# Layer A of a two-layer decoder step: every eighth weight block's low half is subtracted on GpSimd instead of VectorE

## The chip, the core and the metric

The kernel runs on one core of one Trainium2 chip. The metric is the device time of one execution in microseconds (us); lower is better. Five engines run in parallel, each through its own instructions in a fixed order: TensorE (PE, with its weight loads as PEld), VectorE (DVE), ScalarE (ACT), GpSimd (POOL) and SyncE (SP, which here issues the DMA transfers). An instruction waits on semaphores for what it reads and for the buffers that it writes, and everything behind it on its engine waits with it.

## The reference

One inference step of a trunk with two layers, D_MODEL = 2048, branch width 4096, 64 heads of 64. It runs on a prompt of 16 + 256 tokens and on 8 single-token samples, 280 token columns in all, with shared weights, all in fp32. Layer A is RWKV-7 time mixing, layer B window attention. What matters here is layer A:

```python
rkvz = jnp.einsum('btpd,pde->btpe', xm[:, :, :4], w_rkvz)     # four weights, 2048 x 4096 each
r, k, v, z = rkvz[:, :, 0], rkvz[:, :, 1], rkvz[:, :, 2], rkvz[:, :, 3]
...
def rwkv7_step(S, inp):
    r, d, k, v, kk, b = inp
    sa = jnp.einsum('bhij,bhj->bhi', S, kk)
    S = S * d[:, :, None, :] - sa[..., None] * b[:, :, None, :] + v[..., None] * k[:, :, None, :]
    return S, jnp.einsum('bhij,bhj->bhi', S, r)
...
y = y.reshape(B, T, WIDTH).astype(dt) * jax.nn.silu(z)
return y @ w_out, S_fin.astype(S0.dtype), xn[:, -1]
```

The outputs are the normalised rows of prompt and samples, the recurrent and shift states, and the key and value caches.

## The kernel before

**Weights.** Every large product keeps its weights on TensorE in two parts, since an fp32 value is multiplied as a high part and a rest: `whi` is the weight rounded to the type fp32r, and `wlo` is the weight minus `whi`. `mm3` (L218 to L220) then issues three matmuls per tile: `whi` by the high part of the activations (L218), `whi` by their rest (L219), and `wlo` by the high part (L220). Weights come in blocks of 128 partitions x 512 elements: two slices of 128 rows of the weight, 256 columns wide. `wunits` makes one block at a time: a DMA on SP's queue into a tile `raw` (L211, five buffers), and then `split`: ScalarE casts `raw` into `whi` (L195) and VectorE subtracts `raw` minus `whi` into `wlo` (L197). `whi` and `wlo` have five buffers each. A buffer of `raw` is free for its next DMA when both the cast and the subtraction have read it.

**Products.** A product of layer A covers 256 output columns and all 2048 rows of depth, so it consumes eight blocks, numbered in tile names by the row slice they start at (0, 2, ... 14; `wlo_z_14` is the eighth block of a product of z). In the stage that matters here `products` (L709) emits 16 products of r, 12 of k, 12 of v, 16 of z (the first four of k and v are made ahead of it), and eight products of the output projection that are named `oa`: 64 products of eight blocks. Each block gives 12 matmuls. In the trace's names `ps_r`, `ps_k`, `ps_v`, `ps_z`, `ps_o` are the PSUM tiles of these products.

**What runs between.** `drive` (L610) steps through the products and, between the pieces, through streams of other work on each group of heads. `prep` loads k, r and v back from DRAM (`kT`, `kk`, `rT`, `vT`) and makes decays; its L932 copies the eight sample columns of six tiles into a tile `sm` on GpSimd, each as its tile comes in. `prep_e` and `scores` build masked score matrices; at L1064 to L1067 GpSimd masks them (`nd`, `N`, `Noff`). Then VectorE turns one of them around and runs a substitution of 14 steps (`stmp` L1075, `NL` L1077), which ends in the transpose `TN` (L1081). `solve` (L1102, `ps_so`) reads `TN` on TensorE. `chain` carries the state over, and `group_norm` ends with transposes `ps_yt` (L1275) that VectorE evacuates into `vT` (L1276). Eight pairs of head groups go through this.

**What sets the order.** TensorE's order is written by hand: `drive` works inside `pe_order`, and TensorE keeps the order in which the program emits. The order on all other engines is chosen when the program is built, by a scheduler that simulates the engines. A block is made one or more blocks ahead of its use, as far as the five buffers allow.

Of the kernel before, what the change touches and what calls it, by code (L numbers as in the profile page):

```python
# [12 lines left out]
F32 = mybir.dt.float32  # L13
# [3 lines left out]
ALU = mybir.AluOpType  # L17
# [81 lines left out]
class Pools:  # L99


    def __init__(self, pools, tags):
        self.pools, self.tags = pools, tags.split()
# [6 lines left out]
class Kernel:  # L110
    def __init__(self, nc, tc, I, O):
        self.nc, self.tc, self.I, self.O = nc, tc, I, O

        self.raws, self.los = [], []

        self.wx = self.hold = None
        self.behind = []
        self.plan = []
        self.pools = {}
# [69 lines left out]
    def dram(self, name, shape):  # L189
        return self.dp.tile(shape, F32, name=name, tag=name)  # L190

    def split(self, hi, lo, src):

        with self.tc.issue_after(self.root) if self.hold else contextlib.nullcontext():
            self.nc.scalar.copy(hi, src)  # L195
        with self.tc.issue_after(self.hold) if self.hold else contextlib.nullcontext():
            return self.nc.vector.tensor_tensor(lo, src, hi.bitcast(F32), op=ALU.subtract)  # L197

    def wunits(self, w, name, nk, col, nc_, per):

        nc = self.nc
        assert nc_ == 256 and per == 2, (nc_, per)
        for k0 in range(0, nk, per):
            t = lambda n, dt, **k: self.wp.tile([128, 512], dt, tag=n, name=f"{n}_{name}_{col}_{k0}", **k)[
                :, :per * nc_].rearrange("p (k c) -> p k c", k=per)
            if self.wx and len(self.raws) % 2:
                raw = self.wx.tile([128, 512], F32, tag="rawx", bufs=4, name=f"raw_{name}_{col}_{k0}")[
                    :, :per * nc_].rearrange("p (k c) -> p k c", k=per)
            else:
                raw = t("raw", F32, bufs=5)  # L210
            self.raws.append(nc.sync.dma_start(raw.rearrange("p k c -> p (k c)"), w[col // 256, k0 // 2]))  # L211
            hi, lo = t("whi", F32R), t("wlo", F32R)
            self.los.append(self.split(hi, lo, raw))
            yield k0, hi, lo

    def mm3(self, ps, wh, wl, xh, xl, start, stop):
# [392 lines left out]

    def drive(self, products, streams, begun, ahead=2000):  # L610
        self.samples = False
        live = [[g, *begun.get(g, (0, None))] for g in streams]

        now = streams[:2]
        more = True
        with self.pe_order():
            while more or self.later or len(live) > 1:
                for s in list(live):
                    if s[1] <= self.pos and (s[2] is None or s[2]()):

                        turn = self.tc.issue_after(self.los[-2].ins) if self.pos and s[0] not in now else \
                            contextlib.nullcontext()
                        try:
                            with self.tc.high_priority(offset=ahead if s[0] is now[1] else 0), turn:
                                w = next(s[0])
                        except StopIteration:
                            live.remove(s)
                            continue
                        w, need = w if isinstance(w, tuple) else (w, None)
                        s[1:] = [self.pos + w, need]  # L630
                live += [[g, 0, None] for g in self.side]
                self.side = []
                more = more and next(products, None) is not None
                self.pos += 1

    def mark(self, *k):
        self.done[k] = self.pos
# [1335 lines left out]
```

## Time and profile before

| | |
|---|---|
| time, median of 3 runs | 2118.64 us (2115.4 to 2123.16) |
| the profiled execution's own time | 2118.32 us, span 2116.5 us, clock 0.99 |
| TensorE busy | 2064.9 us, 98% of the span |
| VectorE busy | 1697.8 us, 80% |
| ScalarE busy | 1263.8 us, 60% |
| GpSimd busy | 122.5 us, 6%, 188 instructions |

The span is the profiled part of that execution; its own time includes what lies around it, 1.8 us. A row of a timeline gives start and duration in us, the engine, the line, and, in brackets, how long the engine had been idle before the instruction and what ended the idle time. A row of the waits gives the engine and line that waited, after the arrow what it waited for, and then the total in us, how many times, and the longest. Rows of a tile or line give duration in ns (minimum, median, maximum) and the first and the last start. Layer A's products run from about 142 to 1275 us.

### The profile page before, as it was taken

Reading aid. Unit: us, or ns where it says so; the run is one execution under the profiler, and the core shown is the slowest. Engines: PE = TensorE matmul, PEld = TensorE weight load, DVE = VectorE, ACT = ScalarE, POOL = GpSimd, SP = SyncE. Lnnn points to the kernel's source line nnn. Section 1 sums busy time; section 2 is a strip of 40 time slices with the busy share of each in tenths; the row PEclk is TensorE's granted clock in tenths of the full one; section 3 lists DMA queues with packets and bytes.
Section 4 is the critical chain, followed back from the end, with each engine's and each line's share of the span. In section 5 each row is a group of like instructions: output and inputs, shape, how many; then the busy total and the mean of one; then the engine's idle time right before and its main releaser. Section 6 shows DMA issues by size and latency. Waiting matters only on the chain.

```text
span 2116.5 us, 55871 instructions
## 1 busy us (share of the span) xinstructions
PE 2064.9 (98%) x21420; PEld 1965.8 (93%) x21420; DVE 1697.8 (80%) x4112; ACT 1263.8 (60%) x2790; POOL 122.5 (6%) x188
## 2 busy tenths in 40 slices
PE   9999999899999999999999999999999999999997
PEld 7999899889899989899999999999999999999997
DVE  8867777687678878888888788997888888878885
ACT  3457766576766757767676445565565655544443
POOL 0011100001010010100100001100000000000000
PEclk9999999999999999999999999999999999999999
DMA  7898667658756876777657687757455444567774
GB/s 258 314 312 250 189 213 241 188 181 290 216 180 205 260 229 198 211 217 222 203 152 246 207 257 243 247 172 227 132 167 156 146 155 130 181 210 247 232 219 132
DMA packets 276356, 446.28 MB, mean 211 GB/s; under 512 B 54056, under 2 KB 97768, under 8 KB 275696
## 3 DMA queue, kind: packets, MB, share of 16 engines
q1 hardware_dynamic: 275656, 441.66, 66.6%
q8 instruction: 168, 2.75, 0.5%
q10 hardware_dynamic: 432, 1.05, 0.1%
q14 instruction: 100, 0.82, 0.1%
HBM read 381.69 MB, written 65.03 MB: 211 GB/s over the span
## 4 chain that ended last, share of the span: by engine, by line
PE 87%; DVE 5%; ACT 3%; DMA 3%; issue 2%; SPq 0%; POOL 0%; DVEq 0%; POOLq 0%; ACTq 0%
PE ps_z L218 6%; PE ps_z L219 6%; PE ps_z L220 6%; PE ps_k L218 3%; PE ps_ob L218 3%; PE ps_ob L220 3%; PE ps_v L218 3%; PE ps_ob L219 3%; PE ps_r L218 3%; PE ps_q L218 3%; PE ps_q L220 3%; PE ps_q L219 3%; PE ps_k L219 3%; PE ps_k L220 3%; PE ps_v L220 3%; PE ps_v L219 3%
## 5 line engine op out<-in xcount | busy, mean ns | idle before, releaser
L218 PE MATMUL ps_z<-mhlm,whi_z 128*128 128x280 f32 x512 | 158.6, 310 | 2.8 <-ACT sr L937 2.0
L219 PE MATMUL ps_z<-mhlm,whi_z 128*128 128x280 f32 x512 | 150.6, 294 | 0.0
L220 PE MATMUL ps_z<-mhlm,wlo_z 128*128 128x280 f32 x512 | 150.3, 294 | 0.0
L218 PE MATMUL ps_q<-bmh,whi_qb 128*128 128x264 f32 x512 | 150.0, 293 | 0.1
L218 PE MATMUL ps_z<-bmh,whi_zb 128*128 128x264 f32 x512 | 147.4, 288 | 0.0
L220 PE MATMUL ps_q<-bmh,wlo_qb 128*128 128x264 f32 x512 | 145.6, 284 | 0.6 <-DVE wlo_qb L197 0.6
L219 PE MATMUL ps_q<-bml,whi_qb 128*128 128x264 f32 x512 | 145.6, 284 | 0.0
L219 PE MATMUL ps_z<-bml,whi_zb 128*128 128x264 f32 x512 | 145.5, 284 | 0.0
L220 PE MATMUL ps_z<-bmh,wlo_zb 128*128 128x264 f32 x512 | 145.4, 284 | 0.0
L218 PE MATMUL ps_ob<-ghi,whi_ob 128*128 128x264 f32 x512 | 145.3, 285 | 0.0
L220 PE MATMUL ps_ob<-ghi,wlo_ob 128*128 128x264 f32 x512 | 144.6, 284 | 0.0
L219 PE MATMUL ps_ob<-glo,whi_ob 128*128 128x264 f32 x512 | 144.6, 283 | 0.0
L195 ACT CAST whi_ob<-raw_ob 128x512 fp32r<-128x512 f32 x128 | 79.1, 620 | 96.9 <-PE ps_ob L219 77.8
L195 ACT CAST whi_oa<-raw_oa 128x512 fp32r<-128x512 f32 x128 | 79.2, 620 | 88.0 <-PE ps_oa L219 30.6
L197 DVE TENSOR_TENSOR wlo_r<-raw_r,whi_r 128x512 fp32r<-128x512 f32 x128 | 87.8, 691 | 42.6 <-ACT whi_r L195 41.3
L218 PE MATMUL ps_v<-mhlm,whi_v 128*128 128x280 f32 x384 | 119.8, 312 | 0.4 <-ACT st L790 0.4
L218 PE MATMUL ps_k<-mhlm,whi_k 128*128 128x280 f32 x384 | 119.1, 310 | 1.0 <-ACT st L790 1.0
L195 ACT CAST whi_v<-raw_v 128x512 fp32r<-128x512 f32 x128 | 79.0, 619 | 65.8 <-PE ps_v L219 37.7
L197 DVE TENSOR_TENSOR wlo_v<-raw_v,whi_v 128x512 fp32r<-128x512 f32 x128 | 87.3, 687 | 36.9 <-ACT whi_v L195 35.6
L195 ACT CAST whi_zb<-raw_zb 128x512 fp32r<-128x512 f32 x128 | 78.2, 619 | 62.9 <-PE ps_z L219 38.5
L220 PE MATMUL ps_k<-mhlm,wlo_k 128*128 128x280 f32 x384 | 112.4, 293 | 2.1 <-issue 2.1
L219 PE MATMUL ps_v<-mhlm,whi_v 128*128 128x280 f32 x384 | 112.7, 293 | 0.0
(478 smaller groups left out, 7604.1 us busy)
## 6 DMA issues: line engine op xcount, KB each, us to landing
raw_k<-a_w_rkvz SPq DMA_DIRECT2D x128, 256.0 KB
raw_v<-a_w_rkvz SPq DMA_DIRECT2D x128, 256.0 KB
raw_r<-a_w_rkvz SPq DMA_DIRECT2D x128, 256.0 KB
raw_z<-a_w_rkvz SPq DMA_DIRECT2D x128, 256.0 KB
raw_oa<-a_w_out SPq DMA_DIRECT2D x128, 256.0 KB
raw_qb<-b_w_qz SPq DMA_DIRECT2D x128, 256.0 KB
raw_zb<-b_w_qz SPq DMA_DIRECT2D x128, 256.0 KB
raw_ob<-b_w_o SPq DMA_DIRECT2D x128, 256.0 KB
```

The source lines that it names most:

```text
L195: self.nc.scalar.copy(hi, src)
L197: return self.nc.vector.tensor_tensor(lo, src, hi.bitcast(F32), op=ALU.subtract)
L218: mm(ps, wh, xh, start=start, stop=False)
L219: mm(ps, wh, xl, start=False, stop=False)
L220: return mm(ps, wl, xh, start=False, stop=stop)
```

## The change

`drive` sets a flag `turned_over` while it works with `ahead` above zero, which is so in layer A alone. While it is set, `wunits` issues the subtraction of every eighth block on GpSimd instead of VectorE. The cast stays on ScalarE. The whole diff:

```diff
--- before.py
+++ after.py
@@ -114,6 +114,7 @@
         self.raws, self.los = [], []
 
         self.wx = self.hold = None
+        self.turned_over = False
         self.behind = []
         self.plan = []
         self.pools = {}
@@ -189,12 +190,12 @@
     def dram(self, name, shape):
         return self.dp.tile(shape, F32, name=name, tag=name)
 
-    def split(self, hi, lo, src):
+    def split(self, hi, lo, src, engine=None):
 
         with self.tc.issue_after(self.root) if self.hold else contextlib.nullcontext():
             self.nc.scalar.copy(hi, src)
         with self.tc.issue_after(self.hold) if self.hold else contextlib.nullcontext():
-            return self.nc.vector.tensor_tensor(lo, src, hi.bitcast(F32), op=ALU.subtract)
+            return (engine or self.nc.vector).tensor_tensor(lo, src, hi.bitcast(F32), op=ALU.subtract)
 
     def wunits(self, w, name, nk, col, nc_, per):
 
@@ -210,7 +211,8 @@
                 raw = t("raw", F32, bufs=5)
             self.raws.append(nc.sync.dma_start(raw.rearrange("p k c -> p (k c)"), w[col // 256, k0 // 2]))
             hi, lo = t("whi", F32R), t("wlo", F32R)
-            self.los.append(self.split(hi, lo, raw))
+            turn = self.turned_over and len(self.los) % 8 == 7
+            self.los.append(self.split(hi, lo, raw, nc.gpsimd if turn else None))
             yield k0, hi, lo
 
     def mm3(self, ps, wh, wl, xh, xl, start, stop):
@@ -609,6 +611,7 @@
 
     def drive(self, products, streams, begun, ahead=2000):
         self.samples = False
+        self.turned_over = ahead > 0
         live = [[g, *begun.get(g, (0, None))] for g in streams]
 
         now = streams[:2]
@@ -632,6 +635,7 @@
                 self.side = []
                 more = more and next(products, None) is not None
                 self.pos += 1
+        self.turned_over = False
 
     def mark(self, *k):
         self.done[k] = self.pos
```

The eighth block is always the last of its product, so 64 subtractions move, all named `..._14`: VectorE's instructions go from 4078 to 4014 and GpSimd's from 193 to 257 in the program. No matmul changes its place on TensorE. Since the other engines are ordered by the scheduler, other instructions change places too. In the changed file, lines after the first insertions stand one lower (L197 is L198), and those behind `drive` four lower (L1276 is L1280). Three places follow; names carry the tile, the row slice and a number of the tile.

The first is on GpSimd, at the masked scores of the first pair of head groups (at 228 us of the trace): `N` is the masked matrix that the substitution on VectorE begins with, `wlo_r_14` a moved block's rest. Before:

```order
L932 COPY sm_3068<-kk_3043 128x2x8
L932 COPY sm_3068<-Pp 128x2x8
L1067 TENSOR_TENSOR Noff<-F,consts 128x16x16
L1064 TENSOR_TENSOR nd_2955<-F,consts 128x320
L1065 TENSOR_TENSOR nd_2956<-F,consts 128x320
L1066 TENSOR_TENSOR N_1741<-nd_2955,nd_2956 128x320
L932 COPY sm_3068<-kT_3039 128x2x8
```

With the change:

```order
L198 TENSOR_TENSOR wlo_r_14_2779<-raw_r_14_2776,whi_r_14_2778 128x512
L936 COPY sm_3068<-kk_3043 128x2x8
L936 COPY sm_3068<-Pp 128x2x8
L1071 TENSOR_TENSOR Noff<-F,consts 128x16x16
L1068 TENSOR_TENSOR nd_2955<-F,consts 128x320
L1069 TENSOR_TENSOR nd_2956<-F,consts 128x320
L198 TENSOR_TENSOR wlo_r_14_3118<-raw_r_14_3115,whi_r_14_3117 128x512
L1070 TENSOR_TENSOR N_1741<-nd_2955,nd_2956 128x320
L936 COPY sm_3068<-kT_3039 128x2x8
```

Two moved subtractions came in, one of them between the two masked halves `nd` and their sum `N`.

The second is on GpSimd, at the first products of z (877 to 930 us of the trace): the copies into `sm` each follow a load from DRAM. Before:

```order
L932 COPY sm_14370<-kT_14146 128x2x8
L932 COPY sm_14370<-ta_13724 128x2x8
L932 COPY sm_14370<-vT_14368 128x2x8
L932 COPY sm_15116<-vT_15114 128x2x8
L932 COPY sm_15116<-rT_15081 128x2x8
```

With the change:

```order
L936 COPY sm_14370<-kT_14146 128x2x8
L198 TENSOR_TENSOR wlo_z_14_14253<-raw_z_14_14250,whi_z_14_14252 128x512
L936 COPY sm_14370<-ta_13724 128x2x8
L936 COPY sm_14370<-vT_14368 128x2x8
L198 TENSOR_TENSOR wlo_z_14_14507<-raw_z_14_14504,whi_z_14_14506 128x512
L936 COPY sm_15116<-vT_15114 128x2x8
L936 COPY sm_15116<-rT_15081 128x2x8
```

The moved subtractions stand between copies that wait for transfers: `wlo_z_14_14507` is behind the copy of `vT_14368`.

The third is on VectorE, ahead of the evacuation `vT<-ps_yt` at 381 us of the trace. `kk` waits for a load, `stmp_14` and `NL` are the last step of a substitution. Before:

```order
L898 SCALAR_TENSOR_TENSOR kk_5449<-kT_5445,par,kk_5449 128x280
L1075 TENSOR_TENSOR stmp_14_5118<-NL_5077 128x28
L898 SCALAR_TENSOR_TENSOR kk_5449<-kT_5445,par,kk_5449 128x280
L910 SCALAR_TENSOR_TENSOR cl_4871<-reset,cl_4871 128x272 x2
L904 TENSOR_TENSOR kT_5445<-kT_5445,km_4_5454 128x280
L1077 TENSOR_TENSOR NL_5077<-NL_5077,stmp_14_5118 128x2x14
L197 TENSOR_TENSOR wlo_v_14_5425<-raw_v_14_5422,whi_v_14_5424 128x512
L904 TENSOR_TENSOR kT_5445<-kT_5445,km_4_5457 128x280
L906 TENSOR_TENSOR ta_4872<-ta_4872,kk_5449 128x560
L1081 STREAM_TRANSPOSE TN_5123<-NL_5077 128x512
L1082 STREAM_TRANSPOSE TR_5124<-NL_5077 128x512
L1276 SCALAR_TENSOR_TENSOR vT_2043<-ps_yt_0_5399,par,vT_2043 128x272
```

With the change:

```order
L1079 TENSOR_TENSOR stmp_14_5118<-NL_5077 128x28
L1081 TENSOR_TENSOR NL_5077<-NL_5077,stmp_14_5118 128x2x14
L198 TENSOR_TENSOR wlo_v_12_5407<-raw_v_12_5404,whi_v_12_5406 128x512
L902 SCALAR_TENSOR_TENSOR kk_5449<-kT_5445,par,kk_5449 128x280 x2
L1085 STREAM_TRANSPOSE TN_5123<-NL_5077 128x512
L1086 STREAM_TRANSPOSE TR_5124<-NL_5077 128x512
L914 SCALAR_TENSOR_TENSOR cl_4871<-reset,cl_4871 128x272 x2
L908 TENSOR_TENSOR kT_5445<-kT_5445,km_4_5454 128x280
L908 TENSOR_TENSOR kT_5445<-kT_5445,km_4_5457 128x280
L910 TENSOR_TENSOR ta_4872<-ta_4872,kk_5449 128x560
L1280 SCALAR_TENSOR_TENSOR vT_2043<-ps_yt_0_5399,par,vT_2043 128x272
```

`wlo_v_14` is gone from the stretch between `kk` and `vT`, and the last substitution step moved ahead of `wlo_v_12` and `kk`.

## The prediction

> **What bounds the kernel now.** I began with the profile's page. Its first part gives each engine's busy time, its fourth the chain of work that ended last, by engine.
>
> ```profile
> PE 2064.9 (98%) x21420; PEld 1965.8 (93%) x21420; DVE 1697.8 (80%) x4112; ACT 1263.8 (60%) x2790; POOL 122.5 (6%) x188
> PE 87%; DVE 5%; ACT 3%; DMA 3%; issue 2%; SPq 0%; POOL 0%; DVEq 0%; POOLq 0%; ACTq 0%
> ```
>
> TensorE is busy for 98% of the span. VectorE's 80% is the next highest, but it holds only 5% of the chain. The change touches layer A's products, so the second view is that stretch alone, us 142 to 1275, as a table of busy times.
>
> ```profile
> core 0: us, PE busy (x) PEld busy (x) DVE busy (x) ACT busy (x) POOL busy (x), PEclk, DMA share, GB/s
> 142.00:1275.00 1133.00, 1099.23 (x13734) 1034.21 (x13734) 896.39 (x2022) 753.54 (x1664) 84.39 (x137) 0.99 0.70 218
> ```
>
> TensorE is idle there for 1133.00 − 1099.23 = 33.8 us, and runs at 0.99 of its clock. Nothing that this change does can shorten the matmuls, so 33.8 us (1.6% of the kernel) is all there is to win. Which waits make it up is the third view, TensorE's waits in the same stretch; these rows are those of more than 1 us that VectorE or GpSimd ends.
>
> ```profile
> PE ps_yt L1275 <- DVE vT L1276: 8.0, 2, 6.9
> PE ps_so L1102 <- DVE TN L1081: 6.1, 2, 3.5
> PE ps_bo L954 <- DVE vT L955: 1.5, 2, 1.3
> PE ps_sm L935 <- POOL sm L932: 1.2, 1, 1.2
> PE ps_ch L1191 <- DVE X L1227: 1.1, 1, 1.1
> ```
>
> VectorE's part is 8.0 + 6.1 + 1.5 + 1.1 = 16.7 us in seven waits, and no `wlo` is among them. A faster VectorE can win at most 16.7 us here, 0.8%; no long wait of TensorE is for the blocks themselves.
>
> **The change part by part.** *What a moved subtraction frees.* VectorE does 64 fewer. One row of the page gives the duration of such blocks, and two neighbours in the timeline the pitch.
>
> ```profile
> L197 DVE TENSOR_TENSOR wlo_r<-raw_r,whi_r 128x512 fp32r<-128x512 f32 x128 | 87.8, 691 | 42.6 <-ACT whi_r L195 41.3
> 378.29 0.68 DVE L197 TENSOR_TENSOR wlo_v<-raw_v,whi_v 128x512 fp32r<-128x512 f32 x1
> 378.89 0.44 DVE L904 TENSOR_TENSOR kT<-kT,km 128x280 f32<-128x280 f32 x1
> ```
>
> The duration is 0.69 us, but the next instruction starts 378.89 − 378.29 = 0.60 us later, the ends overlap. So 64 × 0.60 = 38.4 us leave VectorE's 896.39.
>
> *What it costs on GpSimd.* No GpSimd subtraction of 512 elements is in the trace. Its two-input operations of other sizes are:
>
> ```profile
> L1869 POOL TENSOR_TENSOR sqacc<-sqacc,sqb x14: 745/788/1287, 1937.4 to 2102.9; 128x264 f32<-128x264 f32 x14
> L1065 POOL TENSOR_TENSOR nd<-F,consts x8: 863/989/1335, 228.5 to 1137.1; 128x320 f32<-128x320 f32 x8
> L1064 POOL TENSOR_TENSOR nd<-F,consts x8: 868/934/1605, 227.7 to 1136.2; 128x320 f32<-128x320 f32 x8
> ```
>
> The undisturbed minima rise by (863 − 745)/56 = 2.1 ns per element, so 512 elements cost about 863 + 192 × 2.1 = 1270 ns. The upper bound is the slowest of these rows plus the same growth, 1605 + 403 = 2.01 us; the lower is 863 ns. I take 1.27, as the minima are closest to an operation left to itself. That adds 64 × 1.27 = 81 us to GpSimd's 84.39 in 1133: it has room.
>
> *What it costs VectorE in turn.* The two engines disturb each other. Two places of the timeline:
>
> ```profile
> 625.49 0.88 POOL L1065 TENSOR_TENSOR nd<-F,consts 128x320 f32<-128x320 f32 x1
> 625.64 1.27 DVE L197 TENSOR_TENSOR wlo_r<-raw_r,whi_r 128x512 fp32r<-128x512 f32 x1 [0.26 <-ACT whi_r L195]
> 1137.14 0.89 POOL L1065 TENSOR_TENSOR nd<-F,consts 128x320 f32<-128x320 f32 x1
> 1137.20 1.38 DVE L197 TENSOR_TENSOR wlo_z<-raw_z,whi_z 128x512 fp32r<-128x512 f32 x1
> ```
>
> A subtraction on VectorE that starts just behind a GpSimd operation takes 1.27 and 1.38 us instead of 0.69: it ends 0.54 us after GpSimd (626.91 against 626.37). Behind a GpSimd operation of 1.27 us, VectorE's instruction would lose at most 1.27 + 0.54 − 0.69 = 1.12 us, and at least nothing, where VectorE happens to be idle, in a one-input operation, or first. I take the two rows' 0.6. So per move VectorE gains between 0.60 and 0.60 − 1.12 = −0.52 us, and by the middle about nothing: 64 moves are worth +38 to −33 us of VectorE's time, near 0. The Trainium skill has this rule in "SBUF — State Buffer", section "Who interferes with whom": a VectorE instruction with two SBUF inputs contends with a GpSimd instruction that reads SBUF, the shared port pair is an exclusive lock for the whole instruction, and whoever came first holds it. By that rule, if every one of the 64 collides at its start, VectorE comes out up to 33 us worse (an estimate), where the two rows' 0.6 gives about nothing; the stretched rows agree that the lock is there.
>
> *Is a moved block late?* A block's rest may come as late as its first L220 matmul. The tightest of the 64, where the cast covers two blocks and the second starts 0.6 us in:
>
> ```profile
> 1022.92 1.14 ACT L195 CAST whi_z<-raw_z 128x512 fp32r<-128x512 f32 x2
> 1027.11 0.29 PE L220 MATMUL ps_z<-mhlm,wlo_z 128*128 128x280 f32 x1
> ```
>
> Its cast ends at 1023.54, so 3.57 us are left; 1.27 us on GpSimd fit, and so do 2.01. The next question is GpSimd's queue, where a moved block stands behind copies that wait for transfers. The longest such wait that I found, by setting the new order of GpSimd on the times of this trace:
>
> ```profile
> 907.67 0.62 ACT L195 CAST whi_z<-raw_z 128x512 fp32r<-128x512 f32 x1 [0.29 <-PE ps_z L219]
> 910.79 0.47 POOL L932 COPY sm<-vT 128x16 f32<-128x16 f32 x1 [12.39 <-DMA vT<-vd]
> 922.17 0.29 PE L220 MATMUL ps_z<-mhlm,wlo_z 128*128 128x280 f32 x1
> ```
>
> The block is cast at 908.29, the copy ahead of it is done at 911.26: 2.97 us late, and then 1.27. It would be ready at 912.5, needed at 922.17. So the blocks cost TensorE nothing: the five buffers hide it, and without that cover a move would cost up to 1.27 + 2.97 us. The copies of `sm` behind a moved block are late by up to 1.27; their reader waited once, for 1.2 us. *The buffers of* `raw` come free later by the same amounts, and SP's queue stands behind that:
>
> ```profile
> SPq L211 <- DVE wlo_r L197: 67.3, 53, 5.3
> DMA raw_r<-a_w_rkvz: 9.2, 7
> ```
>
> SP waits for `wlo` often, but the second row, which lists ScalarE's idle time ahead of its casts, shows that a cast found its block missing only seven times for r; most casts wait for TensorE to free `whi`. Nothing for this.
>
> *The waits of TensorE that VectorE sets.* The longest:
>
> ```profile
> 375.65 0.51 DVE L898 SCALAR_TENSOR_TENSOR kk<-kT,par,kk 128x280 f32<-128x280 f32 x1 [4.24 <-DMA kk<-kr]
> 381.45 0.46 DVE L1276 SCALAR_TENSOR_TENSOR vT<-ps_yt,par,vT 128x272 f32<-128x272 f32 x1
> 381.96 0.47 PE L1275 MATMUL ps_yt<-consts,Y 128*128 128x128 f32 x1 [6.92 <-DVE vT L1276]
> ```
>
> VectorE stood 4.24 us before `kk`, held by a load, and worked through to `vT`. `wlo_v_14` (378.29) leaves this stretch: −0.60. The last substitution step moves ahead of `kk` into the idle 4.24: −0.2, estimated. Most of the 6.92 us is the load, which doesn't change. Gain 0.8. At the second wait of that kind:
>
> ```profile
> 896.88 1.28 DVE L197 TENSOR_TENSOR wlo_z<-raw_z,whi_z 128x512 fp32r<-128x512 f32 x2
> 898.81 0.44 PE L1275 MATMUL ps_yt<-consts,Y 128*128 128x128 f32 x2 [1.06 <-DVE vT L1276]
> ```
>
> one of the two blocks leaves, at most −0.60; if GpSimd takes half of it back, −0.3.
>
> *The substitutions.* Their chain begins on GpSimd and ends in `TN`. Of eight, TensorE waited for two; this is the longer one.
>
> ```profile
> 228.51 1.32 POOL L1065 TENSOR_TENSOR nd<-F,consts 128x320 f32<-128x320 f32 x1
> 229.91 0.97 POOL L1066 TENSOR_TENSOR N<-nd,nd 128x320 f32<-128x320 f32 x1
> 255.14 1.05 DVE L1081 STREAM_TRANSPOSE TN<-NL 128x512 f32<-128x512 f32 x1
> 256.24 0.34 PE L1102 MATMUL ps_so<-TN,Noff 32*32 32x16 f32 x18 [3.50 <-DVE TN L1081]
> ```
>
> Here a moved block now stands between `nd` and `N`: +1.27. Two blocks leave VectorE between 231 and 255: −1.20. Each collision in the chain costs about 0.6, and one to two are likely. I put +0.6 on this chain and as much spread over the others, most of which have slack, together +1.0 with bounds of 0 and 3.
>
> The sum, on the profiled execution's own time: 2118.32 − 0.8 − 0.3 + 1.0 = 2118.2, say 2118. That execution is 0.3 us below the median of the runs shown, so the same number stands for the median.
>
> **The rivals.** *B, the relief counts.* If VectorE's freed 38.4 us fall mainly where it is late, its waits of 16.7 us go away: 2118.3 − 16.7 = 2101.6; half of them, 2110. For it: VectorE is 79% busy in the stretch, and each block it gives up lets the scheduler pull others forward. Against: seven waits at few places, the longest of which hangs on a load, and two blocks at most leave each place.
>
> *C, the lock, slower.* VectorE is busy 79% of the time, so nearly each of 64 GpSimd operations meets it. If VectorE then loses 0.6 to 1.12 us just ahead of work that TensorE wants, and the room that the freed 0.60 makes lies elsewhere, TensorE pays: with 20 places of 0.6 us, +12, 2130; with all 64 at the worst 0.52 net, +33, 2151. It decides from 10.6/64 = 0.17 us reaching TensorE per move. For it: the stretched rows, and handoffs without slack. Against: TensorE waited for VectorE only seven times in the stretch, so most delays of 0.6 us meet slack.
>
> *D, GpSimd's queue.* A moved block is stuck behind copies whose tiles come late, beyond what I replayed from old times:
>
> ```profile
> POOL sm L932 <- DMA rT<-rd: 239.3, 13, 37.7
> POOL sm L932 <- DMA vT<-vd: 109.4, 8, 22.0
> ```
>
> These waits are long, 37.7 us at the most. A block that falls behind a long one stops TensorE for that long less the time between cast and use (3.57 and 13.88 us in the two places above), and holds its `raw` too. If five blocks lose 2 us each: +10, 2128. Against: the scheduler places the blocks by its own times, and on this trace's times the worst wait was 2.97 us.
>
> That the change does nothing is excluded: 64 rows stand on GpSimd in the new order.
>
> **How the numbers follow.** A measurement of this kernel can tell about 0.5%, 10.6 us, from no change: faster is below 2108.0, slower above 2129.2. My forecast, no measurable change with 2118 and 2111 to 2125 of its own: 0.72. B 0.10, of which 0.06 below 2108. C 0.12, of which 0.09 above 2129.2. D 0.06, of which 0.02 above. So faster 0.06, slower 0.11, same 0.83. The range of 2110 to 2129 reaches B at half its worth and D and C at their near ends; about 0.17 is left out.
>
> **What would show it.** `wlo` on GpSimd of 1.2 to 1.4 us where undisturbed. VectorE's busy time in the stretch nearly unchanged or up to 40 us lower, and stretched `wlo` rows of 1.2 to 1.8 us beside GpSimd's. TensorE's idle time there again 30 to 38 us, with L220 not waiting for `wlo` of GpSimd. The wait at 382 near 6 us. I am wrong if TensorE waits for GpSimd's `wlo`, if its waits for `TN` or `vT` reach 25 us or more (C), or fall under 6 (B).

## The result: 0.6% slower

| | median | runs |
|---|---|---|
| before | 2118.36 us | 2115.40 to 2123.16 (6) |
| changed | 2131.12 us | 2127.89 to 2135.86 (6) |

The ratio is 1.0058, with a 95% interval of 1.0040 to 1.0076: 12.8 us slower by the medians. The forecast of 2118 was wrong, and the time lies above the range of 2110 to 2129. The profiled execution of the changed kernel took 2127.89 us, with a span of 2126.0: 9.5 us more than the span before. Its page, busy times and chain:

```profile
PE 2064.1 (97%) x21420; PEld 1962.8 (92%) x21420; DVE 1683.8 (79%) x4048; ACT 1263.1 (59%) x2790; POOL 211.7 (10%) x252
PE 79%; DVE 9%; DMA 5%; ACT 3%; issue 3%; SPq 1%; POOL 0%; DVEq 0%; POOLq 0%; ACTq 0%
```

TensorE does the same work (2064.1 us against 2064.9), and VectorE is busy 14.0 us less. Yet VectorE's share of the chain has gone from 5% to 9%. Layer A now ends some 9 us later, so its stretch is 142 to 1284:

```profile
142.00:1284.00 1142.00, 1099.40 (x13734) 1032.56 (x13733) 882.38 (x1958) 752.64 (x1664) 172.94 (x202) 0.99 0.70 217
```

TensorE is idle for 1142.00 − 1099.40 = 42.6 us, where it was 33.8. Its waits in that stretch: all that VectorE ends and that come to more than 1 us in sum, and the largest that ScalarE ends.

```profile
PE ps_yt L1279 <- DVE vT L1280: 12.2, 7, 5.9
PE ps_ch L1209 <- ACT W L1200: 4.5, 4, 2.1
PE ps_so L1106 <- DVE TN L1085: 3.9, 2, 3.5
PE ps_ch L1195 <- DVE X L1231: 3.7, 2, 2.2
PE ps_bo L958 <- DVE vT L959: 1.2, 2, 0.9
```

The waits that VectorE ends add up to 21.0 us in 13 places, where they were 16.7 in seven. The two longest, 5.9 and 3.5 us, stood there before as well (6.9 and 3.5). The new ones are of 3.1 us at most, along the state chain (`ps_ch`) and the group norms (`ps_yt`). ScalarE's wait in the state chain has grown too; before it was:

```profile
PE ps_ch L1205 <- ACT W L1196: 1.3, 2, 0.9
```

No wait of TensorE there is for GpSimd. The granted clock isn't the cause: over the whole span it is 0.990 before and 0.992 changed. The loss isn't spread evenly. Matched by the order of TensorE's matmuls, which is the same in both, the two traces can be cut at the same two places. Before, and then changed:

```profile
142.00:921.00 779.00, 749.84 (x9256) 703.59 (x9256) 593.46 (x1349) 528.45 (x1182) 67.70 (x108) 0.98 0.71 220
921.00:1277.00 356.00, 351.39 (x4516) 332.63 (x4504) 304.19 (x677) 225.96 (x485) 16.69 (x29) 1.00 0.68 213
```

```profile
142.00:912.00 770.00, 746.53 (x9297) 699.57 (x9296) 581.96 (x1304) 527.51 (x1182) 123.49 (x151) 0.99 0.71 222
912.00:1286.00 374.00, 354.87 (x4475) 334.98 (x4463) 301.55 (x657) 225.80 (x484) 49.45 (x51) 0.99 0.67 206
```

Up to the first products of z the changed kernel is 9 us ahead (770 us for what took 779). In the rest of layer A it loses 18 (374 against 356), 12 of them in the last 77 us: what starts at 1200 us before starts 2.5 us earlier in the changed kernel, what starts at 1277 starts 9.2 us later. One of the places where it loses, the last step of the state chain, before:

```profile
1225.24 0.29 DVE L1227 COPY X<-FS 64x256 f32<-64x256 f32 x1
```

and changed, on three engines:

```profile
1228.21 1.26 POOL L198 TENSOR_TENSOR wlo_oa<-raw_oa,whi_oa 128x512 fp32r<-128x512 f32 x1 [7.65 <-ACT whi_oa L196]
1228.34 1.29 DVE L1231 COPY X<-FS 64x256 f32<-64x256 f32 x1
1229.68 0.62 PE L1195 MATMUL ps_ch<-X,E 128*16 128x64 f32 x14 [1.50 <-DVE X L1231]
```

A copy of 0.29 us starts 0.13 us behind a moved subtraction, takes 1.29 us, and TensorE stands for 1.50 us. That is what rival C calls the lock. But the order on VectorE is new too, so the trace alone doesn't say what the lock costs in all.

### The profile page after: what moved, and what is told of

It reads as the page before. It is cut to its first block, busy times and chain, and to the rows that moved or that the text cites. A ratio compares the mean times of both kernels' runs of the same rounds, so it can differ in the third digit from the quotient of the medians.

```text
span 2126.0 us, 55879 instructions
## 1 busy us (share of the span) xinstructions
PE 2064.1 (97%) x21420; PEld 1962.8 (92%) x21420; DVE 1683.8 (79%) x4048; ACT 1263.1 (59%) x2790; POOL 211.7 (10%) x252
## 4 chain that ended last, share of the span: by engine, by line
PE 79%; DVE 9%; DMA 5%; ACT 3%; issue 3%; SPq 1%; POOL 0%; DVEq 0%; POOLq 0%; ACTq 0%
PE ps_z L220 5%; PE ps_z L221 5%; PE ps_z L222 5%; PE ps_v L220 3%; PE ps_ob L220 3%; PE ps_ob L222 3%; PE ps_ob L221 3%; PE ps_q L220 3%; PE ps_q L222 3%; PE ps_q L221 3%; PE ps_k L220 3%; PE ps_v L221 3%; PE ps_v L222 3%; PE ps_r L220 2%; PE ps_k L221 2%
## 5 line engine op out<-in xcount | busy, mean ns | idle before, releaser
L220 PE MATMUL ps_k<-mhlm,whi_k 128*128 128x280 f32 x384 | 119.1, 310 | 0.8 <-issue 0.8
L196 ACT CAST whi_v<-raw_v 128x512 fp32r<-128x512 f32 x128 | 79.0, 619 | 63.2 <-PE ps_v L221 42.6
L222 PE MATMUL ps_v<-mhlm,wlo_v 128*128 128x280 f32 x384 | 112.2, 292 | 0.0
L221 PE MATMUL ps_k<-mhlm,whi_k 128*128 128x280 f32 x384 | 112.2, 292 | 0.0
L198 DVE TENSOR_TENSOR wlo_ob<-raw_ob,whi_ob 128x512 fp32r<-128x512 f32 x128 | 87.3, 692 | 31.3 <-ACT whi_ob L196 30.6
```

Of the source, the lines that this page charges most:

```text
L198: return (engine or self.nc.vector).tensor_tensor(lo, src, hi.bitcast(F32), op=ALU.subtract)
L220: mm(ps, wh, xh, start=start, stop=False)
L221: mm(ps, wh, xl, start=False, stop=False)
L222: return mm(ps, wl, xh, start=False, stop=stop)
```

## The experiments

**Holding the order.** Two things changed at once: the engine of 64 subtractions, and the scheduler's order of everything else. To part them, some kernels below pin the order. A function adds order edges (no waits) between neighbours on each engine, along an order that is written into the kernel as places in the traced program:

```diff
+def keep_order(nc, tc):
...
+    L = list(nc.cur_bb.bb.instructions)
+    dep = mybir.DependencyInfo(mybir.DependencyClass.NoSync, mybir.DependencyReason.DATA)
+    for e, packed in ORDER.items():          # Pool, Activation, DVE, SP
...
+                tc.add_manual_dep(i, before.name, dep, reason="keep_order")
...
         Kernel(nc, tc, I, O).run()
+        keep_order(nc, tc)
```

"Old order" means that all instructions but the edited ones stand as in the kernel before; TensorE's order is the same everywhere. All ratios are to the kernel before, run on the same chip at the same time, with 95% intervals. The runs were made in four sets (e1 to e4, e5 to e8, e9 to e11, e12), so runs of different sets are compared by their ratios and not by their times.

| | subtractions of the 64 blocks | order of the rest | median, us | ratio |
|---|---|---|---|---|
| change | GpSimd | new | 2131.12 | 1.0058 (1.0040 to 1.0076) |
| e1 | GpSimd | old | 2125.61 | 1.0034 (1.0021 to 1.0047) |
| e2 | VectorE | new | 2126.52 | 1.0045 (1.0029 to 1.0061) |
| e3 | none, GpSimd writes zeros | old | 2113.77 | 0.9979 (0.9965 to 0.9992) |
| e9 | none, GpSimd writes zeros three times | old | 2114.38 | 0.9978 (0.9965 to 0.9991) |
| e10 | none, GpSimd copies | old | 2116.26 | 0.9991 (0.9976 to 1.0006) |
| e7 | GpSimd, in four pieces | old | 2127.63 | 1.0048 (1.0031 to 1.0065) |
| e8 | GpSimd, 128 blocks | old | 2134.65 | 1.0079 (1.0063 to 1.0095) |
| e4 | GpSimd, r, k and v only | scheduler's | 2123.65 | 1.0022 (1.0008 to 1.0035) |
| e5 | GpSimd | scheduler's, streams held | 2126.35 | 1.0041 (1.0026 to 1.0056) |
| e6 | VectorE | scheduler's, streams let go | 2127.35 | 1.0053 (1.0036 to 1.0071) |
| e11 | VectorE | scheduler's, streams held later | 2121.26 | 1.0017 (1.0006 to 1.0028) |
| e12 | VectorE, and the masks too | old | 2120.60 | 1.0010 (1.0001 to 1.0019) |

**e1: the move at the old order.** The changed kernel with the order pinned to that of before.

> The 64 subtractions are on GpSimd, but every engine is held to the order of the kernel before: the remaining instructions of VectorE, ScalarE, GpSimd and SyncE stand exactly as they did there (TensorE's too). So this is the move without the new order. Theory LOCK (GpSimd's 1.27 us stretch VectorE's two-input instructions ahead of work that TensorE waits for): the loss stays, 2128 to 2133 us. Theory ORDER (the 12.7 us come from the places that the scheduler gave the other instructions): the loss is gone, 2112 to 2120, by the relief rather a little under the time before.

Measured: 1.0034. Between the two theories' numbers, nearer to LOCK: the move alone costs 7 us, not 12.8. The interval just meets that of the change (1.0047 and 1.0040), so that both theories hold in part rests on e2 as well.

**e2: the new order without the move.** The kernel before, pinned to the changed kernel's order; the 64 subtractions go where the scheduler puts them between.

```diff
-turn = self.tc.issue_after(self.los[-2].ins) if self.pos and s[0] not in now else \
+turn = self.tc.issue_after(self.los[-2].ins) if self.pos and s[0] not in now and not (
+    ahead > 0 and len(self.los) % 8 == 1) else \
```

> The counterpart: all subtractions are on VectorE, as before, but the other instructions of VectorE, ScalarE, GpSimd and SyncE are held to the order of the changed kernel; the 64 subtractions stand on VectorE where the scheduler puts them between those. So this is the new order without the move. LOCK: about the time before, 2116 to 2122. ORDER: the loss is here, 2126 to 2136.

Measured: 1.0045. ORDER's number. The new order is dear by itself. The two costs, 0.34% and 0.45%, make 0.79%, more than the change's 0.58%; the intervals are too wide to say whether they add up.

**e3: the relief without the reading.**

```diff
-self.los.append(self.split(hi, lo, raw, nc.gpsimd if turn else None))
+if turn:
+    nc.scalar.copy(hi, raw)
+    self.los.append(nc.gpsimd.memset(lo.bitcast(F32), 0.0))
+else:
+    self.los.append(self.split(hi, lo, raw))
```

> As the first run (order of the kernel before on all engines), but GpSimd writes zeros into the 64 blocks' rests instead of subtracting, so it reads nothing; the 64 rests are left out of the products. VectorE has the same relief, and nothing on GpSimd reads beside it. LOCK: 10 to 18 us under the first run, 2108 to 2118. ORDER: within 3 us of the first run, 2112 to 2120, since the lock then cost nothing there either.

Measured: 0.9979, 11.8 us under e1: LOCK's number. (The time of 2113.8 alone would lie in both ranges.) It differs from e1 only in what GpSimd does in the 64 blocks. So taking 64 subtractions from VectorE is worth 0.21%, 4.5 us, and GpSimd's doing them costs 0.55%, 11.7 us. A memset is shorter than a subtraction, reads nothing and doesn't wait for the cast. e9 and e10 ask which of these counts, for the length and the reading.

**e9: GpSimd as long busy, without reading.** Against e3:

```diff
-    self.los.append(nc.gpsimd.memset(lo.bitcast(F32), 0.0))
+    for q in range(3):
+        part = nc.gpsimd.memset(lo.bitcast(F32), 0.0)
...
+    self.los.append(part)
```

> As the third run of the first set (64 rests written as zeros by GpSimd, order of the kernel before, the rests left out of the products), with three memsets for each block, 3 x 0.5 us, so that GpSimd is occupied at least as long as by a subtraction, yet reads nothing. If it is GpSimd's reading that costs: 2110 to 2118, as with one memset (2113.8). If it is how long GpSimd is busy, or that its blocks come late: 2120 to 2127.

**e10: reading one input.** Against e3:

```diff
-    self.los.append(nc.gpsimd.memset(lo.bitcast(F32), 0.0))
+    self.los.append(nc.gpsimd.tensor_copy(lo, raw))
```

> The same frame, with one copy of the raw block into the rest on GpSimd: one input read instead of two (the products then take the raw weight for the rest, which leaves the subtraction out). If any reading by GpSimd stops VectorE's two-input instructions: well over the memset runs, 2119 to 2126, in proportion to the copy's length. If only GpSimd's two-input operations do: 2111 to 2117.

Measured: 0.9978 for the memsets, as with one of them: how long GpSimd is busy costs nothing that can be measured. 0.9991 for the copies, 2116.3: by the time, the second number, and not clear of the memsets. But a copy is short, and VectorE shows it below. GpSimd's rows (line, operation, tiles, shape, count, then busy us and mean ns, then its idle time) of the memsets and of the copies:

```profile
L219 POOL MEMSET wlo_r<- 128x512 f32 x48 | 25.2, 526 | 108.5 <-PE ps_r L231 106.9
```

```profile
L217 POOL CAST wlo_r<-raw_r 128x512 fp32r<-128x512 f32 x16 | 10.8, 677 | 108.0 <-PE ps_r L226 88.7 <-DMA raw_r<-a_w_rkvz 13.6 <-DMA kk<-kr 5.8
```

Three memsets take 1.58 us a block, more than a subtraction's 1.29 (the median); a copy takes 0.68 on the average. VectorE's busy time on the pages of e1, e3, e9 and e10 says the same from the other side:

```profile
PE 2068.1 (97%) x21420; PEld 1967.1 (93%) x21420; DVE 1682.5 (79%) x4048; ACT 1263.4 (59%) x2790; POOL 207.9 (10%) x252
```

```profile
PE 2060.6 (98%) x21420; PEld 1961.7 (93%) x21420; DVE 1658.8 (79%) x4048; ACT 1264.5 (60%) x2790; POOL 151.9 (7%) x252
```

```profile
PE 2060.9 (97%) x21420; PEld 1963.3 (93%) x21420; DVE 1658.7 (78%) x4048; ACT 1265.1 (60%) x2790; POOL 220.6 (10%) x380
```

```profile
PE 2062.9 (98%) x21420; PEld 1964.4 (93%) x21420; DVE 1665.2 (79%) x4048; ACT 1263.7 (60%) x2790; POOL 168.6 (8%) x252
```

All four have the same VectorE instructions in the same order. With memsets they take 1658.7 and 1658.8 us, with copies 1665.2, with subtractions 1682.5. So a subtraction on GpSimd stretches VectorE's instructions by (1682.5 − 1658.8)/64 = 0.37 us on the average, a copy by 0.10. The Trainium skill's rule ("SBUF — State Buffer", section "Who interferes with whom": GpSimd instructions that read SBUF contend with VectorE's two-input ones, those that only write don't) agrees with all four. The zeros in e3 aren't the whole reason for its lead over e1: e10 has none, and its interval ends where that of e1 has not begun (1.0006 and 1.0021). In e1 it isn't lateness of the blocks either, as TensorE's waits there show no `wlo` of GpSimd; its largest:

```profile
PE ps_yt L1279 <- DVE vT L1280: 8.5, 5, 6.3
PE ps_so L1106 <- DVE TN L1085: 6.8, 2, 3.5
PE ps_so L1112 <- issue: 5.3, 2, 3.3
PE ps_ch L1209 <- ACT W L1200: 3.5, 3, 1.6
```

The same waits in e3:

```profile
PE ps_yt L1283 <- DVE vT L1284: 8.5, 4, 6.0
PE ps_so L1110 <- DVE TN L1089: 6.4, 2, 3.9
PE ps_so L1116 <- issue: 3.1, 1, 3.1
PE ps_ch L1213 <- ACT W L1204: 1.4, 2, 1.0
```

So TensorE's waits that VectorE ends hardly differ (in sum 19.0 us in e1 and 17.6 in e3); what grew are those that ScalarE ends (12.2 and 6.8). The way from VectorE's stretched instructions to TensorE is therefore not seen in one kind of wait, and it stays open. One rival was not run by itself: a subtraction also waits for its cast, so it can hold GpSimd's queue and its buffers longer than the memsets and the copies do. The traces speak against it: in e1 no wait of TensorE or of ScalarE in layer A is ended by GpSimd, and ScalarE's casts stood for a missing block for 22 us, against 24 in e3.

**e7: four pieces.** Each GpSimd subtraction of e1 cut into four of 128 elements.

```diff
+for q in range(4):
+    cut = lambda x: x[:, q // 2, 128 * (q % 2):128 * (q % 2) + 128]
+    part = nc.gpsimd.tensor_tensor(cut(lo), cut(raw), cut(hi).bitcast(F32), op=ALU.subtract)
...
```

> The move at the order of the kernel before, with each GpSimd subtraction cut into four of 128 elements (estimate from the 264- and 320-element rows: 0.46 us each, 1.84 us for a block). The lock is held per instruction, so VectorE should lose at most one piece's time per instruction. If what TensorE pays is the longest single hold: 2115 to 2121. If it pays for all of GpSimd's reading time: 2126 to 2132, a little over the uncut run (2125.6).

Measured: 1.0048, the second number. GpSimd's groups for the blocks of r, in e7 and in e1:

```profile
L220 POOL TENSOR_TENSOR wlo_r<-raw_r,whi_r 128x128 fp32r<-128x128 f32 x64 | 34.6, 572 | 105.8 <-ACT whi_r L217 92.4 <-DMA vecd<-sr 13.3
```

```profile
L198 POOL TENSOR_TENSOR wlo_r<-raw_r,whi_r 128x512 fp32r<-128x512 f32 x16 | 21.6, 1349 | 107.7 <-ACT whi_r L196 80.1 <-DMA vt<-N 14.0 <-DMA vecd<-sr 13.3
```

A block takes 4 x 0.57 = 2.29 us in pieces and 1.35 whole. VectorE's busy time in e7 is 1674.3 us:

```profile
PE 2065.9 (97%) x21420; PEld 1965.7 (93%) x21420; DVE 1674.3 (79%) x4048; ACT 1265.9 (60%) x2790; POOL 254.9 (12%) x444
```

So the pieces stretch VectorE by less, (1674.3 − 1658.8)/64 = 0.24 us a block against 0.37, though the whole reading has become longer; and the kernel isn't faster for it. Against e1 the intervals overlap, so that e7 is dearer isn't shown.

**e8: twice as many.** e1 with `% 4 == 3` in place of `% 8 == 7`; in `drive`, the streams are not queued behind moved blocks, and the order is pinned as in e1.

> The move doubled, to every fourth block (128 subtractions on GpSimd), all else at the order of the kernel before. LOCK with a price per move: the first run's +0.34% (7 us) doubles to +14, 2131 to 2137. If the relief of VectorE grows and the lock's price was paid at a few unlucky places: 2120 to 2128.

Measured: 1.0079, 2.3 times the cost of e1: a price per move, not a few unlucky places.

**e4: r, k and v alone.** The changed kernel with one condition more:

```diff
-turn = self.turned_over and len(self.los) % 8 == 7
+turn = self.turned_over and len(self.los) % 8 == 7 and name in ("r", "k", "v")
```

> As the changed kernel, with the scheduler free, but only the 40 eighth blocks of r, k and v are subtracted on GpSimd; those of z and oa stay on VectorE. The traces of before and of the change show the changed kernel ahead by 9 us at the beginning of z (921 us of before's trace) and behind by 9 us at the end of oa (1277). If what is lost there belongs to the moves of z and oa: 2107 to 2114. If the gain and the loss are accidents of one order, anything from 2114 to 2128. LOCK by itself says a loss in proportion to the moves, 40 of 64: 2126.

Measured: 1.0022, inside the wide second number and a miss of the first: the 9 us that the changed kernel was ahead at z are not there when the later moves are left out. At that place e4's trace is 5 us behind that of before. They belonged to one order of the program, and e4 has another. LOCK's 2126 for 40 moves lies inside e4's interval, so e4 doesn't speak against it.

**Why the order is dear: e5 and e6.** `drive` queues the instructions of most streams behind the last subtraction but one (`issue_after(self.los[-2].ins)`). That function queues an instruction only if it stands on the engine of the subtraction that is named. Where that subtraction has gone to GpSimd, the streams' VectorE instructions are queued behind nothing (and their GpSimd instructions behind the moved subtraction). So the change also loosens VectorE's order at every eighth block. e5 is the change with the streams held to the last subtraction on VectorE:

```diff
+held = -3 if ahead > 0 and len(self.los) % 8 == 1 else -2
-turn = self.tc.issue_after(self.los[-2].ins) if ...
+turn = self.tc.issue_after(self.los[held].ins) if ...
```

> The changed kernel, scheduler free, with one difference in drive: streams are queued behind the last subtraction that stands on VectorE. (issue_after queues an instruction only on the engine of the subtraction it names; where that one has moved to GpSimd, the streams' VectorE instructions are queued behind nothing, so the change also loosened the order on VectorE at every eighth block.) If the new order's cost of some 5 to 9 us (the second run of the first set gave +0.45%) comes from that loosening: 2123 to 2128, as the run that moves at the old order (2125.6). If it comes from the scheduler's places in general: 2128 to 2134, as the change.

e6 is the kernel before with the streams let go at those blocks:

```diff
+free = ahead > 0 and len(self.los) % 8 == 1
-turn = self.tc.issue_after(self.los[-2].ins) if self.pos and s[0] not in now else \
+turn = self.tc.issue_after(self.los[-2].ins) if self.pos and s[0] not in now and not free else \
```

> The kernel before, all subtractions on VectorE and the scheduler free, but at every eighth block the streams are queued behind nothing, as the change does without saying so. If the loosened queue is what made the new order dear: 2124 to 2130. If not: 2116 to 2122.

Measured: 1.0053 for e6, the first number. Nothing moved engines there; letting go of the streams alone costs as much as e2's new order. TensorE's largest waits in e6:

```profile
PE ps_yt L1276 <- DVE vT L1277: 11.6, 4, 8.3
PE ps_so L1103 <- DVE TN L1082: 6.1, 2, 3.5
PE ps_ch L1206 <- ACT W L1197: 4.7, 5, 2.1
PE ps_sm L936 <- POOL sm L933: 3.6, 1, 3.6
```

Two of these, `ps_yt` and `ps_ch`, grew in the changed kernel as well. e5 came to 1.0041, the number that was expected if the loosening is the cause, and near e1. But its interval overlaps that of the change, so e5 alone doesn't part the two.

The traces say more. Of VectorE's 3072 instructions that are no block subtractions, 137 stand out of their old order in the changed kernel (counted against the longest order that both traces have in common). With the hold kept, in e5, 129 still do, and e5 differs from the changed kernel in 34. So the hold brings little of the old order back. e6's order differs from that of before in 66 and from that of the change in 116: it is a third order, which costs as much. That letting go of the streams costs 0.53% in the kernel before is measured; that it is what made the change's order dear is not shown.

**e11: holding later still.** The kernel before with `self.los[-1]` in place of `self.los[-2]`.

> The kernel before, all subtractions on VectorE, with the streams queued behind the last block's subtraction instead of the last but one: the queue tightened where the change loosened it. If the price of the loosened queue (about 0.5%) is a price of letting streams go ahead of blocks, tightening may win: 2108 to 2116. If the place was at its best already: 2118 to 2130.

Measured: 1.0017, the second number. No gain; the place was better as it was. With all subtractions on VectorE, each of the three other orders that were run was slower than that of before: e2, e6 and e11, by 0.17 to 0.53%. So the order of before may simply be a good one from which most changes lose. No run rules that out.

**e12: the other way round.** The kernel before with GpSimd's 32 two-input operations of layer A put on VectorE, the rest at the old order:

```diff
-G.tensor_tensor(t1, ND[:, :, 0:16], mask(0, 20), op=MU)
+V.tensor_tensor(t1, ND[:, :, 0:16], mask(0, 20), op=MU)
```

and so for `t2`, `N16` and `Noff`.

> The opposite direction: in the kernel before, the 32 two-input GpSimd operations that are already there in layer A (nd, nd, N, Noff; 0.86 to 1.6 us each on GpSimd) go to VectorE, the other instructions at the order of the kernel before. If GpSimd's reading beside VectorE is what costs, and a shorter start of the substitutions helps the two waits for TN: 2109 to 2117. If the 32 x 0.45 us (estimated from VectorE's rows of 320 and 280 elements) that VectorE gains weigh more: 2119 to 2126.

Measured: 1.0010, 2120.6, at the lower end of the second number: less of GpSimd's reading doesn't pay where VectorE has to do the work instead (it is busy 1704.7 us, 6.9 more). No version that computes everything was faster than the kernel before.

## Why the prediction was wrong, step by step

- **What bounds the kernel** was right: TensorE's work is unchanged, and what VectorE's relief can win is small. e3 and e9 put it at 4.5 us, of the 16.7 that were named as the most. Rival B fell with that.
- **GpSimd's price** was right: 1.27 us were estimated. The row of the changed kernel:

```profile
L198 POOL TENSOR_TENSOR wlo_z<-raw_z,whi_z x16: 1272/1294/3443, 875.1 to 1143.0; 128x512 fp32r<-128x512 f32 x16
```

- The upper bound of 2.01 was too low: three of the 64 took longer (2.29, 3.36 and 3.44 us), the longest beside VectorE instructions that followed each other without a gap. No wait of TensorE is for these blocks.
- **The blocks' lateness** at nothing was right, and rival D did not happen.
- **The wait at 382** was put at 6.92 − 0.8 = 6.1; it came out at 5.92:

```profile
379.39 0.49 DVE L1280 SCALAR_TENSOR_TENSOR vT<-ps_yt,par,vT 128x272 f32<-128x272 f32 x1
379.94 0.90 PE L1279 MATMUL ps_yt<-consts,Y 128*128 128x128 f32 x3 [5.92 <-DVE vT L1280]
```

- **The step that failed first** is the term "+1.0 with bounds of 0 and 3" for collisions. It was mis-sized: e1 against e3 gives 11.7 us. The gains, −0.8 and −0.3, were mis-sized too, but by less: e3 gives 4.5 us. The balance behind the term was even kinder than assumed, as a moved subtraction takes 0.37 us of VectorE on the average and not 0.6, and VectorE came out 14 us ahead. The mistake was to weigh the freed and the lost time of VectorE as if a microsecond of each had the same price. By e3 the 39.0 us that leave VectorE's busy time are worth 4.5 us, 0.12 for one. By e1 against e3 the 23.7 us of stretching cost 11.7, 0.5 for one; by e7 against e3 the 15.5 us cost 14.6, 0.9 for one. So stretching is dearer than freed time; that it has a fixed price per microsecond is not shown. In the places looked at, what is freed is a block's subtraction, which had slack, and what is stretched can be an instruction that TensorE stands waiting for, such as the 0.29 us copy of the state chain. That copy has one input, a kind that the lower bound counted as free. That this explains the whole difference in price is an inference; the prices are measured.
- **The step that was missing** is the new order as a cost of its own. The prediction read the order at three places for what left and what came, and put the rest at nothing without a reason. By e2 the order alone costs 0.45%, 9.5 us. The prediction also missed that `issue_after` loses its grip on VectorE when the block it names is on GpSimd. Whether that is why the order is dear stays open, and so does how much of the change's 0.58% is the order and how much the collisions.
- **Rival C** had the time, 2130, and its threshold of 0.17 us per move was passed by the change as a whole (12.8/64 = 0.20). But by e1 the move alone costs 7/64 = 0.11, so a part of that is the order. C was given 0.12, against seven waits with slack elsewhere. Its mechanism is shown by e1, e3, e8 and e9, but it isn't the only one. Its sign did not come: the waits for `TN` and `vT` are 12.2 + 3.9 + 1.2 = 17.3 us, and 25 were named. TensorE's idle time in the stretch, 42.6 us where 30 to 38 were named, did show that the forecast was wrong.

## What to carry to other kernels

An engine's freed time and the time that it loses to a neighbour don't cancel: freed time counts where TensorE waits, while a collision can hit a short instruction in a serial chain, if it is of a kind that is held up. Here, beside a VectorE that is busy 80% of the time, subtractions on GpSimd had a price that grew with their number; cutting them in pieces didn't lower it, and writing alone cost nothing that could be measured. Before an instruction changes engines, look at what names it: an order edge that holds on one engine only is gone after the move. And a move in a scheduled kernel is two changes, of the engine and of the order: to price the move, pin the order and move the work alone.

## What the runs showed of the hardware

A one-input copy on VectorE (64x256, 0.29 us) was stretched to 1.29 behind a GpSimd subtraction, so it isn't two-input instructions alone. But it isn't all instructions. Of VectorE's instructions that began inside a moved subtraction in the changed kernel, 25 of 39 with two tiles of SBUF as inputs took over 0.1 us longer than their median. All 30 that read PSUM, all 7 reductions and all 3 transposes kept their length to 0.03 us. A place with two of these, which take 0.68 us elsewhere too:

```profile
921.89 1.40 POOL L198 TENSOR_TENSOR wlo_z<-raw_z,whi_z 128x512 fp32r<-128x512 f32 x1 [0.98 <-ACT whi_z L196]
922.07 0.67 DVE L1318 TENSOR_REDUCE dsa<-dT 128x8 f32<-128x512 f32 x1
922.77 0.68 DVE L1128 COPY ET<-ps_so 32x512 f32<-32x512 f32 x1
```

The holding goes both ways: a GpSimd subtraction of 1.27 us took 3.44 us while VectorE issued one instruction after the other, most of them with two inputs.

And a wait of TensorE can cost more than itself. In the changed kernel, one wait, and the busy times of the 5 us around it and of stretches behind it (columns as in the tables of stretches above):

```profile
1264.88 0.90 PE L1279 MATMUL ps_yt<-consts,Y 128*128 128x128 f32 x3 [3.07 <-DVE vT L1280]
...
1260.00:1265.00 5.00, 1.93 (x16) 1.71 (x15) 5.00 (x8) 1.24 (x3) 2.29 (x1) 0.91 1.05 397
1265.00:1270.00 5.00, 5.00 (x22) 5.00 (x23) 4.41 (x8) 2.49 (x4) 0.00 (x0) 0.50 1.07 324
...
1275.00:1280.00 5.00, 5.00 (x41) 5.00 (x40) 1.83 (x3) 2.16 (x4) 1.10 (x1) 1.00 0.93 304
```

The granted clock (the number behind GpSimd's column) is 0.50 for the next 5 us, in which TensorE does 22 matmuls; at a clock of 1.00 it does 41. That is about 2.5 us more, an estimate from half the rate over 5 us. The kernel before had the same at another place, which the changed kernel has not:

```profile
913.43 0.78 PE L1102 MATMUL ps_so<-TN,Noff 32*32 32x16 f32 x43 [2.56 <-DVE TN L1081]
...
915.00:920.00 5.00, 5.00 (x47) 4.93 (x40) 1.28 (x3) 2.87 (x5) 0.20 (x1) 0.53 0.79 247
```

Not every wait does it: in the kernel before, the clock stayed at 1.00 from 862 to 867 us, behind a wait of 2.03 us. So part of what a new order costs or brings at one place is where such a wait falls. Over the whole span it comes to nothing here, with 0.990 and 0.992.
